# Another order for the half products of an MLP's down projection, with later weight differences and other banks for the last transposes

## The chip, the cores and the metric

The kernel runs on one core of one Trainium2 chip, as one launch. The metric is the device time of a whole execution in microseconds (us), lower is better. All data are float32.

## What is computed

A decoder trunk of two layers on 512 tokens of width 1024. In each layer a normalised input goes through one wide projection and three token mixers (latent attention, RWKV-7, short convolution), whose gated sum goes through an output projection into the residual. Then comes the MLP, which the change touches:

```python
h2 = rms_norm(x, mlp_norm[l])
x = x + jnp.square(jax.nn.relu(h2 @ w_up[l])) @ w_down[l]      # w_up 1024 x 4096, w_down 4096 x 1024
```

## The kernel before

**Exact products from two halves.** TensorE multiplies in a reduced float32 format (fp32r). So every operand is split in a high half, a cast on ACT, and a low half, the rest, a subtraction on DVE. A product of 128 x 128 by 128 x 512 is three matmuls: high by high, high by low, low by high. For weights this happens in split_block (L247 the cast, L248 the low half) and in weights() (L261, L262), for activations in split_into (L339, L340). The halves of weights lie in a ring of four pairs of buffers. Weights come by DMA in blocks of 256 KB, issued on SyncE's queue.

**The MLP in quarters.** Each layer's MLP has four quarters q. A quarter makes 1024 of the 4096 hidden columns: eight up-projection products in the order 0, 4, 1, 5, 2, 6, 3, 7 (UP_ORDER; n_ counts them), each evacuated by two ACT instructions (L1303, L1304). With each of m = 4 to 7 a block j = 0 to 3 of the hidden activations is complete. DVE then forms four half-width sums and differences of it (L1311, L1314, L1312, L1315, in the order in which they stand on DVE), and the results are split.

**Seven half products.** The down projection of a quarter is done in the Strassen-Winograd way: 7 products of quadrants in place of 8. The activations' quadrant operands are A11, S1, S2, S3, S4, A12, A22. The weight quadrants wa, wb, wc, wd hold four blocks each; room gives them the tiles col, kql, ext, z, rstd and mg: wa and wb are col blocks and one kql, wc is three kql and ext, wd is z, z, rstd and mg. These tiles serve the mixers too, under the same names. Three quadrants come by DMA (down_block, L1271). DVE computes wd = wc - wb (L1324) and wb = wb - wa (L1325) once the weights are there. The function less (L1359) makes a further difference of a quadrant while the products run: wc - wb ahead of S2, and the fourth quadrant less wb ahead of A22. The fourth quadrant's own weights are loaded late, into wd, each block after S3's split of that block is done.

Each product is 24 matmuls of 128 x 128 by 128 x 512 (L1344, L1345, L1346) into two PSUM banks, one for each half (t) of 256 tokens: px (pool "g"), pz ("a") or yp ("b"). In program order these are A11 px, S1 pz, S2 px, S3 px, S4 pz, A12 yp, A22 px. What a product leaves in px or pz is added to accumulators ya by add_out: on DVE (L1277), or in an accumulator's first use on ACT (L1279). A product that writes a bank waits until the bank's last result has been added.

**The end of a layer.** In the last quarter the accumulators are finished one by one. finish(b, dh) transposes four 128 x 128 pieces on TensorE into a bank of pool "c" (L1286), DVE adds them to the residual tile am (L1288), and a DMA stores it (L1290) to a spill or the output. In the last quarter A22 runs its two token halves one after the other (by_tokens), with finish(0,0) and finish(1,0) between them.

**What sets the order.** Each engine runs its instructions in the order in which they were put there. A scheduler sets it when the kernel is built, from its own model of times, priorities (tc.high_priority) and the program's order. So an instruction of the MLP can stand among the mixers' work, as the weight differences do: they need only the loaded weights.

Of the kernel before, what the change touches and what calls it, by code (L numbers as in the profile page):

```python
# [22 lines left out]
ALU = mybir.AluOpType  # L23
# [3 lines left out]
P = 128  # L27
# [148 lines left out]
def trunk(tc, w, wkv, wq, xin, pos, pp, sm, rg, out, sizes):  # L176
# [29 lines left out]
    V, A, G = nc.vector, nc.scalar, nc.gpsimd  # L206
# [320 lines left out]
    for l in range(NL):  # L527
# [751 lines left out]
                A.activation(out=ya[b][dh], in_=pd, func=AF.Copy, scale=r_)  # L1279
            seen.add((b, dh))  # L1280

        def finish(b, dh):

            pf = pt("c", (P, 4, P))
            for i in range(4):
                nc.tensor.transpose(pf[:, i], ya[b][dh][:, i * P:(i + 1) * P], ident)  # L1286
            part = xt[:, 4 * dh:4 * dh + 4, b * P:(b + 1) * P]
            V.tensor_tensor(out=part, in0=pf, in1=part, op=ALU.add)  # L1288
            dst = xd if l < NL - 1 else out
            nc.sync.dma_start(out=dst.rearrange("p (k t) -> p k t", t=T)[:, 4 * dh:4 * dh + 4, b * P:(b + 1) * P], in_=part)  # L1290

        for q in range(4):
# [3 lines left out]
            for n_, m in enumerate(UP_ORDER):  # L1296
                pu = pt("c")
                run(gemm_steps(pu, None, h2), h2_steps if (q, n_) == (0, 1) else None)
                if (q, n_) == (0, 2):
                    r2 = const.tile([P, NB], F32, name=f"r2_{l}")  # L1300
                    V.tensor_tensor(out=r2, in0=h2_at[0], in1=h2_at[0], op=ALU.mult)
                rl = tl("inv")
                A.activation(out=rl, in_=pu, func=AF.Relu)  # L1303
                A.activation(out=rl, in_=rl, func=AF.Square)  # L1304
                us[m] = rl
                if m >= 4:
                    j = m - 4
                    ua, ub = us.pop(j), us.pop(m)
                    split_into(act["A11", j], ua[:, H1])
                    s12, s34 = tl("inv"), tl("inv")  # L1310
                    V.tensor_tensor(out=s12[:, H1], in0=ua[:, H2], in1=ub[:, H2], op=ALU.add)  # L1311
                    V.tensor_tensor(out=s12[:, H2], in0=s12[:, H1], in1=ua[:, H1], op=ALU.subtract)  # L1312
                    split_into(act["S1S2", j], s12)
                    V.tensor_tensor(out=s34[:, H1], in0=ua[:, H1], in1=ua[:, H2], op=ALU.subtract)  # L1314
                    V.tensor_tensor(out=s34[:, H2], in0=ub[:, H1], in1=s12[:, H2], op=ALU.subtract)  # L1315
                    split_into(act["S3S4", j], s34)
                    split_into(act["A12A22", j], ub)

                if n_ < 6:
                    for i in (2 * n_, 2 * n_ + 1):  # L1320
                        down_block(i, (wa + wb + wc)[i])
                elif n_ == 6:
                    for j in range(4):
                        V.tensor_tensor(out=wd[j], in0=wc[j], in1=wb[j], op=ALU.subtract)  # L1324
                        V.tensor_tensor(out=wb[j], in0=wb[j], in1=wa[j], op=ALU.subtract)  # L1325
            wpos[0], wpos[1] = first + 32, sum(sizes[:first + 32]) * P
            px, pz = [pt("g") for _ in range(2)], [pt("a") for _ in range(2)]

            def product(a, blocks, acc, start, outs, before=None, after=None, by_tokens=False):

                ws = {}
                for t, j in [(t, j) for t in range(2) for j in range(4)] if by_tokens else \
                        [(t, j) for j in range(4) for t in range(2)]:
                    if j not in ws:
                        if before:
                            before(j)
                        ws[j] = split_block(blocks[j])
                        if after:
                            after(j)
                    hi, lo = ws[j]  # L1340
                    ah, al = act[a, j]
                    c = slice(t * P, (t + 1) * P)

                    mm(acc[t], ah[:, c], hi, start=(start and j == 0), stop=False, skip_group_check=True)  # L1344
                    mm(acc[t], ah[:, c], lo, start=False, stop=False, skip_group_check=True)  # L1345
                    mm(acc[t], al[:, c], hi, start=False, stop=(j == 3), skip_group_check=True)  # L1346
                    if by_tokens and j == 3:
                        for th, dh in outs:
                            add_out(acc[t], 2 * th + t, dh)
                        if t == 0:  # L1350
                            finish(0, 0)
                            finish(1, 0)
                if not by_tokens:
                    for t in range(2):
                        for th, dh in outs:
# [6 lines left out]
            product("A11", wa, px, True, [(0, 0)])  # L1362
            product("S1", wb, pz, True, [(1, 1)])
            product("S2", wb, px, False, [(0, 1)], before=less(wb, wc, wb))
            product("S3", wd, px, False, [(1, 1)], after=lambda j: down_block(12 + j, wd[j]))
            product("S4", wc, pz, False, [(0, 1)])
            if last:
                finish(2, 1)
                finish(3, 1)
            product("A12", wd, yp, q == 0, [(0, 0)] if last else [])  # L1370
            if last:
                finish(0, 1)
                finish(1, 1)
            product("A22", wb, px, False, [(1, 0)], before=less(wb, wd, wb), by_tokens=last)
        finish(2, 0)
        finish(3, 0)
        xsrc = xd
    es.close()

# [18 lines left out]
```

## Time and profile before

| | |
|---|---|
| median of 3 runs | 1577.67 us (1577.0 to 1578.12) |
| profiled execution | 1579.63 us |
| its span, first to last instruction | 1577.6 us |
| TensorE (PE) busy | 1559.8 us, 99% |
| DVE busy | 1179.4 us, 75% |
| ACT busy | 797.2 us, 51% |
| GpSimd (POOL) busy | 182.2 us, 12% |
| granted TensorE clock | 0.999 |
| moved by DMA | 156.27 MB, 99 GB/s on the mean |

How to read it: PE is TensorE's matmuls, PEld its weight loads, SPq SyncE's DMA queue. A timeline's row has the start, the duration, the engine, the line, the operation and its tiles (out<-in), and in brackets how long the engine was idle before it and what released it. The duration of a matmul is longer than the distance of two starts, since matmuls are pipelined and their ends are modelled. A waits' row has the total in us, the count and the longest.

### The profile page before, as it was taken

Reading aid. Unit: us, or ns where it says so; the run is one execution under the profiler, and the core shown is the slowest. Engines: PE = TensorE matmul, PEld = TensorE weight load, DVE = VectorE, ACT = ScalarE, POOL = GpSimd, SP = SyncE. Lnnn points to the kernel's source line nnn. Section 1 sums busy time; section 2 is a strip of 40 time slices with the busy share of each in tenths; the row PEclk is TensorE's granted clock in tenths of the full one; section 3 lists DMA queues with packets and bytes.
Section 4 is the critical chain, followed back from the end, with each engine's and each line's share of the span. In section 5 each row is a group of like instructions: output and inputs, shape, how many; then the busy total and the mean of one; then the engine's idle time right before and its main releaser. Section 6 shows DMA issues by size and latency. Waiting matters only on the chain.

```text
span 1577.6 us, 22682 instructions
## 1 busy us (share of the span) xinstructions
PE 1559.8 (99%) x7910; PEld 1259.6 (80%) x7910; DVE 1179.4 (75%) x2351; ACT 797.2 (51%) x1708; POOL 182.2 (12%) x192
## 2 busy tenths in 40 slices
PE   9999999999999999999999999999999999999998
PEld 7888778877788888878777887788778888788786
DVE  8889677688756767686968996776887576776767
ACT  5433556454446554646434335654544565646462
POOL 1312014101100000000022221151111000000000
PEclk9999999999999999999999999999999999999999
DMA  5323324314332424242233243242143324242412
GB/s 180 98 74 112 113 71 143 89 41 167 101 96 79 127 73 133 81 121 67 69 107 92 81 135 93 65 141 74 54 165 98 97 77 128 73 132 74 127 34 80
DMA packets 90786, 156.27 MB, mean 99 GB/s; under 512 B 10032, under 2 KB 20272, under 8 KB 90160
## 3 DMA queue, kind: packets, MB, share of 16 engines
q1 hardware_dynamic: 90672, 154.83, 32.8%
q8 instruction: 62, 1.02, 0.3%
q14 instruction: 52, 0.43, 0.1%
HBM read 145.87 MB, written 8.91 MB: 98 GB/s over the span
## 4 chain that ended last, share of the span: by engine, by line
PE 91%; DVE 5%; DMA 2%; ACT 1%; issue 0%; SPq 0%; DVEq 0%
PE pg L298 12%; PE pg L300 12%; PE pg L302 12%; PE pc L300 7%; PE pc L298 7%; PE pc L302 7%; PE pg L1344 3%; PE pg L1345 3%; PE pg L1346 3%; PE pa L1171 2%; PE pa L1345 1%; PE pa L1346 1%; PE pa L1344 1%; DVE mg L1277 1%; DVE lo L248 1%; PE pc L1197 1%
## 5 line engine op out<-in xcount | busy, mean ns | idle before, releaser
L261 ACT CAST hi<-raw 128x512 fp32r<-128x512 f32 (+1 forms) x366 | 224.6, 618 | 332.7 <-PE pg L300 150.0
L262 DVE TENSOR_TENSOR lo<-raw,hi 128x512 fp32r<-128x512 f32 (+1 forms) x366 | 264.7, 725 | 123.9 <-ACT hi L261 122.0
L300 PE MATMUL pg<-xg,hi 128*128 128x512 f32 x608 | 246.9, 406 | 0.0
L298 PE MATMUL pg<-xg,hi 128*128 128x512 f32 x608 | 245.4, 404 | 0.7 <-DVE z L611 0.7
L302 PE MATMUL pg<-xg,lo 128*128 128x512 f32 x608 | 241.0, 396 | 0.0
L302 PE MATMUL pc<-xg,lo 128*128 128x512 f32 x512 | 199.4, 389 | 0.0
L300 PE MATMUL pc<-xg,hi 128*128 128x512 f32 x512 | 199.2, 389 | 0.0
L298 PE MATMUL pc<-xg,hi 128*128 128x512 f32 x512 | 199.2, 389 | 0.0
L298 PEld LDWEIGHTS pg<-xg,hi 128*128 128x128 f32 x608 | 114.3, 188 | 28.5 <-issue 3.0
L302 PEld LDWEIGHTS pg<-xg,lo 128*128 128x128 f32 x608 | 114.4, 188 | 26.2 <-issue 3.4
L300 PEld LDWEIGHTS pg<-xg,hi 128*128 128x128 f32 x608 | 114.4, 188 | 25.7 <-issue 3.4
L300 PEld LDWEIGHTS pc<-xg,hi 128*128 128x128 f32 x512 | 96.1, 188 | 20.1
L298 PEld LDWEIGHTS pc<-xg,hi 128*128 128x128 f32 x512 | 96.1, 188 | 20.0
L302 PEld LDWEIGHTS pc<-xg,lo 128*128 128x128 f32 x512 | 96.1, 188 | 19.8
L247 ACT CAST hi<-col 128x512 fp32r<-128x512 f32 x104 | 64.6, 621 | 78.9 <-PE pc L300 30.8
L248 DVE TENSOR_TENSOR lo<-col,hi 128x512 fp32r<-128x512 f32 x104 | 71.4, 688 | 34.2 <-ACT hi L247 33.7
L345 POOL TENSOR_TENSOR t<-t,mhalf 128x4 f32<-128x4 f32 (+1 forms) x26 | 46.3, 1783 | 228.1 <-DVE t L356 201.3
L1175 ACT ACTIVATE inv<-pa,t 128x128 f32<-128x128 f32 (+3 forms) x64 | 33.7, 527 | 47.6 <-DVE t L1173 46.1
L247 ACT CAST hi<-kql 128x512 fp32r<-128x512 f32 x48 | 29.8, 622 | 34.3 <-PE pg L1346 24.9
L665 POOL TENSOR_TENSOR mg<-mg,z 128x512 f32<-128x512 f32 x16 | 22.8, 1426 | 180.8 <-DVE z L618 180.8
L612 ACT ACTIVATE z<-z 128x512 f32<-128x512 f32 x48 | 30.3, 632 | 25.0 <-DVE z L611 16.1
L611 DVE TENSOR_TENSOR z<-pg,rstd 128x512 f32<-128x512 f32 x48 | 33.0, 687 | 13.0 <-PE pg L302 10.0
(468 smaller groups left out, 3452.4 us busy)
## 6 DMA issues: line engine op xcount, KB each, us to landing
raw<-in_w_dram SPq DMA_DIRECT2D x364, 256.0 KB, 2.6
col<-in_w_dram SPq DMA_DIRECT2D x56, 256.0 KB, 2.7
kql<-in_w_dram SPq DMA_DIRECT2D x32, 256.0 KB, 2.7
z_spill<-z SPq DMA_DIRECT2D x16, 256.0 KB, 3.3
inv<-z_spill SPq DMA_DIRECT2D x16, 256.0 KB, 5.7
z<-in_w_dram SPq DMA_DIRECT2D x16, 256.0 KB, 2.7
raw<-in_wq_dram SPq DMA_DIRECT2D x12, 192.0 KB, 2.3
am<-in_x_dram SPq DMA_DIRECT2D x8, 256.0 KB, 5.6
```

What stands on the lines that cost most here:

```text
L247: A.copy(hi, src)
L248: V.tensor_tensor(out=lo, in0=src, in1=hi, op=ALU.subtract)
L261: A.copy(hi[:, c], raw[:, c])
L262: V.tensor_tensor(out=lo[:, c], in0=raw[:, c], in1=hi[:, c], op=ALU.subtract)
L298: mm(dst, hi[:, c0:c0 + P], ah, start=(k == 0), stop=False)
L300: mm(dst, hi[:, c0:c0 + P], al, start=False, stop=False)
L302: mm(dst, lo[:, c0:c0 + P], ah, start=False, stop=(k == n - 1))
L345: G.tensor_tensor(out=y, in0=v, in1=mhalf.to_broadcast([P, n]), op=ALU.pow)
L1175: A.activation(out=pe[:, 0:n], in_=psc[:, 0:n], func=AF.Exp, bias=nm[:, h:h + 1], accum_out=rsum[:, h:h + 1])
L1344: mm(acc[t], ah[:, c], hi, start=(start and j == 0), stop=False, skip_group_check=True)
L1345: mm(acc[t], ah[:, c], lo, start=False, stop=False, skip_group_check=True)
L1346: mm(acc[t], al[:, c], hi, start=False, stop=(j == 3), skip_group_check=True)
```

## The change

Four edits, all in the MLP:

1. The program order of the half products becomes A11, S1, S2, S4, S3, A12, A22, with the same banks. The fourth quadrant's weights are loaded into wc, after S4's splits, and A12 and A22's difference use wc.
2. The eight differences of a quarter (now L1327 and L1328) may be issued only after the first difference of block j = 2 (mark).
3. In the last quarter finish(0,1) and finish(1,1) stand before A12, finish(2,1) and finish(3,1) after it; finish(1,0) moves from the middle of A22 to its end. The last three transposes take banks of pools "a", "c", "a"; finish(0,0) keeps "c".
4. finish's add on DVE (now L1289) has high priority.

The lines behind an edit move: the four differences of a block L1311, L1314, L1312, L1315 are L1312, L1315, L1313, L1316 after, the matmuls L1344 to L1346 are L1347 to L1349, and less's L1359 is L1361.

```diff
-        def finish(b, dh):
+        def finish(b, dh, pst="c"):
-            pf = pt("c", (P, 4, P))
+            pf = pt(pst, (P, 4, P))
...
-            V.tensor_tensor(out=part, in0=pf, in1=part, op=ALU.add)
+            with tc.high_priority():
+                V.tensor_tensor(out=part, in0=pf, in1=part, op=ALU.add)
...
-                    V.tensor_tensor(out=s12[:, H1], in0=ua[:, H2], in1=ub[:, H2], op=ALU.add)
+                    mark = V.tensor_tensor(out=s12[:, H1], in0=ua[:, H2], in1=ub[:, H2], op=ALU.add)
...
                 elif n_ == 6:
-                    for j in range(4):
-                        V.tensor_tensor(out=wd[j], in0=wc[j], in1=wb[j], op=ALU.subtract)
-                        V.tensor_tensor(out=wb[j], in0=wb[j], in1=wa[j], op=ALU.subtract)
+                    with tc.issue_after(mark.ins):
+                        for j in range(4):
+                            V.tensor_tensor(out=wd[j], in0=wc[j], in1=wb[j], op=ALU.subtract)
+                            V.tensor_tensor(out=wb[j], in0=wb[j], in1=wa[j], op=ALU.subtract)
...
                         if t == 0:
                             finish(0, 0)
-                            finish(1, 0)
...
             product("S2", wb, px, False, [(0, 1)], before=less(wb, wc, wb))
-            product("S3", wd, px, False, [(1, 1)], after=lambda j: down_block(12 + j, wd[j]))
-            product("S4", wc, pz, False, [(0, 1)])
+            product("S4", wc, pz, False, [(0, 1)], after=lambda j: down_block(12 + j, wc[j]))
+            product("S3", wd, px, False, [(1, 1)])
+            if last:
+                finish(0, 1)
+                finish(1, 1)
+            product("A12", wc, yp, q == 0, [(0, 0)] if last else [])
             if last:
                 finish(2, 1)
                 finish(3, 1)
-            product("A12", wd, yp, q == 0, [(0, 0)] if last else [])
-            if last:
-                finish(0, 1)
-                finish(1, 1)
-            product("A22", wb, px, False, [(1, 0)], before=less(wb, wd, wb), by_tokens=last)
-        finish(2, 0)
-        finish(3, 0)
+            product("A22", wb, px, False, [(1, 0)], before=less(wb, wc, wb), by_tokens=last)
+        finish(1, 0, "a")
+        finish(2, 0, "c")
+        finish(3, 0, "a")
```

**DVE in the third block.** The rows are from the second quarter of layer 0, where block j = 2 is formed (inv_6000 and inv_6001 are its sums and differences, mix, prep, ar hold the halves of the activations, col_4987 on are blocks of wa). Before:

```order
L1311 TENSOR_TENSOR inv_6000<-inv_5953,inv_5995 128x256
L1314 TENSOR_TENSOR inv_6001<-inv_5953 128x256
L1312 TENSOR_TENSOR inv_6000<-inv_6000,inv_5953 128x256
L340 TENSOR_TENSOR ar_4974<-inv_5995,ar_4973 128x512
L1315 TENSOR_TENSOR inv_6001<-inv_5995,inv_6000 128x256
L248 TENSOR_TENSOR lo_6121<-col_4987,hi_6120 128x512
L340 TENSOR_TENSOR prep_4971<-inv_6000,prep_4970 128x512
L340 TENSOR_TENSOR ar_4973<-inv_6001,prep_4972 128x512
L248 TENSOR_TENSOR lo_6131<-col_4988,hi_6130 128x512
L340 TENSOR_TENSOR ar_4974<-inv_6051,ar_4974 128x256
```

and after:

```order
L1327 TENSOR_TENSOR z_4999<-kql_4995,col_4991 128x512
L1327 TENSOR_TENSOR z_5000<-kql_4996,col_4992 128x512
L1327 TENSOR_TENSOR rstd_5001<-kql_4997,col_4993 128x512
L1327 TENSOR_TENSOR mg_5002<-ext_4998,kql_4994 128x512
L1313 TENSOR_TENSOR inv_6000<-inv_6000,inv_5953 128x256
L340 TENSOR_TENSOR ar_4974<-inv_5995,ar_4973 128x512
L248 TENSOR_TENSOR lo_6121<-col_4987,hi_6120 128x512
L1328 TENSOR_TENSOR col_4991<-col_4991,col_4987 128x512
L1328 TENSOR_TENSOR col_4992<-col_4992,col_4988 128x512
L1328 TENSOR_TENSOR col_4993<-col_4993,col_4989 128x512
L1328 TENSOR_TENSOR kql_4994<-kql_4994,col_4990 128x512
L1316 TENSOR_TENSOR inv_6001<-inv_5995,inv_6000 128x256
```

The eight weight differences stand in two groups of four behind the block's first two differences (L1312, L1315) and between its last two (L1313, L1316); these first two stand just ahead of the rows.

**DVE where S4 and S3 are prepared.** In the same quarter, from the add_out of S2's first bank on (pg_6116 and pg_6117 are px, pa_6118 and pa_6119 are pz; z_4999 to mg_5002 are wd, kql_4995 to ext_4998 are wc, col_4991 to kql_4994 are wb). Before:

```order
L1277 SCALAR_TENSOR_TENSOR mg_4980<-pg_6116,r_0_5149,mg_4980 128x512
L248 TENSOR_TENSOR lo_6273<-rstd_5001,hi_6272 128x512
L1277 SCALAR_TENSOR_TENSOR mg_4982<-pg_6117,r_0_5149,mg_4982 128x512
L1359 TENSOR_TENSOR col_4991<-z_4999,col_4991 128x512
L248 TENSOR_TENSOR lo_6284<-mg_5002,hi_6283 128x512
L1359 TENSOR_TENSOR col_4992<-z_5000,col_4992 128x512
L1359 TENSOR_TENSOR col_4993<-rstd_5001,col_4993 128x512
L248 TENSOR_TENSOR lo_6297<-kql_4995,hi_6296 128x512
L248 TENSOR_TENSOR lo_6307<-kql_4996,hi_6306 128x512
L1359 TENSOR_TENSOR kql_4994<-mg_5002,kql_4994 128x512
L1277 SCALAR_TENSOR_TENSOR mg_4984<-pg_6116,r_0_5149,mg_4984 128x512
L248 TENSOR_TENSOR lo_6317<-kql_4997,hi_6316 128x512
```

and after:

```order
L1277 SCALAR_TENSOR_TENSOR mg_4980<-pg_6116,r_0_5149,mg_4980 128x512
L248 TENSOR_TENSOR lo_6273<-kql_4997,hi_6272 128x512
L1277 SCALAR_TENSOR_TENSOR mg_4982<-pg_6117,r_0_5149,mg_4982 128x512
L1361 TENSOR_TENSOR col_4991<-kql_4995,col_4991 128x512
L248 TENSOR_TENSOR lo_6284<-ext_4998,hi_6283 128x512
L1361 TENSOR_TENSOR col_4992<-kql_4996,col_4992 128x512
L248 TENSOR_TENSOR lo_6297<-z_4999,hi_6296 128x512
L1361 TENSOR_TENSOR col_4993<-kql_4997,col_4993 128x512
L248 TENSOR_TENSOR lo_6307<-z_5000,hi_6306 128x512
L1361 TENSOR_TENSOR kql_4994<-ext_4998,kql_4994 128x512
L1277 SCALAR_TENSOR_TENSOR mg_4980<-pa_6118,r_0_5149,mg_4980 128x512
L248 TENSOR_TENSOR lo_6317<-rstd_5001,hi_6316 128x512
```

The add_outs of S2 keep their place. S4's low halves stand where S3's were and S3's where S4's were, and the differences for A22 (L1361) now stand between S3's low halves.

**DVE at the layer change.** From add_out of (2,0) on (mg_4983; mg_4985 is (3,0)); xg, inv and raw belong to the next layer's start. Before:

```order
L1277 SCALAR_TENSOR_TENSOR mg_4983<-pg_7524,r_0_5149,mg_4983 128x512
L1288 TENSOR_TENSOR am_4586<-pc_7849,am_4586 128x4x128
L326 SCALAR_TENSOR_TENSOR xg_7891<-am_4586,pp_82,xg_7890 128x512
L1288 TENSOR_TENSOR am_4586<-pc_7856,am_4586 128x4x128
L384 TENSOR_TENSOR inv_7927<-inv_7923,inv_7925 128x512
L326 SCALAR_TENSOR_TENSOR xg_7895<-am_4586,pp_82,xg_7894 128x512
L262 TENSOR_TENSOR lo_7959<-raw_7957,hi_7958 128x512
L384 TENSOR_TENSOR inv_7931<-inv_7927,inv_7929 128x512
L1277 SCALAR_TENSOR_TENSOR mg_4985<-pg_7525,r_0_5149,mg_4985 128x512
```

and after:

```order
L1277 SCALAR_TENSOR_TENSOR mg_4983<-pg_7524,r_0_5149,mg_4983 128x512
L1289 TENSOR_TENSOR am_4586<-pc_7849,am_4586 128x4x128
L326 SCALAR_TENSOR_TENSOR xg_7891<-am_4586,pp_82,xg_7890 128x512
L384 TENSOR_TENSOR inv_7927<-inv_7923,inv_7925 128x512
L326 SCALAR_TENSOR_TENSOR xg_7895<-am_4586,pp_82,xg_7894 128x512
L262 TENSOR_TENSOR lo_7959<-raw_7957,hi_7958 128x512
L1277 SCALAR_TENSOR_TENSOR mg_4985<-pg_7525,r_0_5149,mg_4985 128x512
L384 TENSOR_TENSOR inv_7931<-inv_7927,inv_7929 128x512
L1289 TENSOR_TENSOR am_4586<-pa_7869,am_4586 128x4x128
```

The add_out of (3,0) stands two rows further forward: one final add and one L384 that stood ahead of it now follow it.

**DVE at the end of layer 1's attention.** L618 and L340 belong to the mixers' sum, raw and lo to its weights; z, rstd, col and kql in the rows L1324 and L1325 are the first quarter's weights. Before:

```order
L1202 TENSOR_TENSOR prep_11119<-pc_12026,prep_11118 128x128
L1324 TENSOR_TENSOR z_12677<-kql_12673,col_12669 128x512
L618 SCALAR_TENSOR_TENSOR inv_12057<-inv_12057,pg_12059 128x512
L1325 TENSOR_TENSOR col_12669<-col_12669,col_12665 128x512
L262 TENSOR_TENSOR lo_12157<-raw_12155,hi_12156 128x512
L1324 TENSOR_TENSOR rstd_12678<-kql_12674,col_12670 128x512
L618 SCALAR_TENSOR_TENSOR inv_12083<-inv_12083,pg_12085 128x512
L340 TENSOR_TENSOR ar_12073<-mg_9780,ar_12073 128x512
L1325 TENSOR_TENSOR col_12670<-col_12670,col_12666 128x512
L262 TENSOR_TENSOR lo_12184<-raw_12182,hi_12183 128x512
L618 SCALAR_TENSOR_TENSOR inv_12109<-inv_12109,pg_12111 128x512
```

and after:

```order
L1202 TENSOR_TENSOR prep_11119<-pc_12026,prep_11118 128x128
L618 SCALAR_TENSOR_TENSOR inv_12057<-inv_12057,pg_12059 128x512
L262 TENSOR_TENSOR lo_12157<-raw_12155,hi_12156 128x512
L618 SCALAR_TENSOR_TENSOR inv_12083<-inv_12083,pg_12085 128x512
L340 TENSOR_TENSOR ar_12073<-mg_9780,ar_12073 128x512
L262 TENSOR_TENSOR lo_12184<-raw_12182,hi_12183 128x512
L618 SCALAR_TENSOR_TENSOR inv_12109<-inv_12109,pg_12111 128x512
```

The rows L1324 and L1325 are gone from between the mixers' rows; the same rows are gone from layer 0's attention.

## The prediction

> **What bounds the kernel now.** I read the page first: the busy shares and the engines of the chain that ended last.
>
> ```profile
> PE 1559.8 (99%) x7910; PEld 1259.6 (80%) x7910; DVE 1179.4 (75%) x2351; ACT 797.2 (51%) x1708; POOL 182.2 (12%) x192
> PE 91%; DVE 5%; DMA 2%; ACT 1%; issue 0%; SPq 0%; DVEq 0%
> ```
>
> TensorE sets the time, and the change leaves its matmuls in number and size as they are. So only TensorE's standstills can go, and they are short. Next I read PE's own waits (columns: us in total, times, longest):
>
> ```profile
> PE pg L1344 <- DVE mg L1277: 2.9, 12, 0.3
> PE pc L1286 <- DVE mg L1277: 2.2, 2, 1.8
> ```
>
> Twelve waits of the products' first matmuls (L1344) for add_out (L1277) are two in each of six quarters: the first quarter of a layer has no L1277 yet. The timeline shows what such a wait costs in full. Here is PE in the second quarter of layer 0, at the end of S1 (bank pa), in S2 (pg), and where S3 (pg again) begins:
>
> ```profile
> 586.53 0.39 PE L1344 MATMUL pa<-hi,ar 128*128 128x512 f32 x1
> 587.02 0.50 PE L1345 MATMUL pa<-lo,ar 128*128 128x512 f32 x1
> ...
> 588.31 0.39 PE L1344 MATMUL pg<-hi,mix 128*128 128x512 f32 x1
> ...
> 591.05 0.39 PE L1344 MATMUL pg<-hi,prep 128*128 128x512 f32 x1
> 591.35 0.50 PE L1345 MATMUL pg<-lo,prep 128*128 128x512 f32 x1
> ...
> 593.79 0.40 PE L1346 MATMUL pg<-hi,ar 128*128 128x512 f32 x1
> 594.42 0.47 PE L1344 MATMUL pg<-hi,mix 128*128 128x512 f32 x1 [0.24 <-DVE mg L1277]
> 594.73 0.39 PE L1345 MATMUL pg<-lo,mix 128*128 128x512 f32 x1
> 594.95 0.40 PE L1346 MATMUL pg<-hi,mix 128*128 128x512 f32 x1
> 595.59 0.50 PE L1344 MATMUL pg<-hi,mix 128*128 128x512 f32 x1 [0.24 <-DVE mg L1277]
> 595.93 0.39 PE L1345 MATMUL pg<-lo,mix 128*128 128x512 f32 x1
> ```
>
> Durations overlap, so I count start to start. S2's 23 steps from 588.31 to 593.79 take 5.48 us, stall included, so an undisturbed step is about 0.23. Of the stalls, (a) is 587.02 - 586.53 - 0.23 = 0.26, where PE wants the low half (L248) of S1's fourth weight block; (b) is 0.30 - 0.23 = 0.07, for the low half of S2's third block; (c) is the S2-to-S3 change: 0.63, 0.31, 0.64 and 0.34 less 0.23 each, 0.40 + 0.08 + 0.41 + 0.11 = 1.00 us. A matmul after a stall also comes about 0.1 late, so (a) and (b) count 0.11 more each, 0.55 together. In the first quarter of a layer add_out runs on ACT (L1279), and (c) is smaller:
>
> ```profile
> 511.06 0.39 PE L1346 MATMUL pg<-hi,ar 128*128 128x512 f32 x1
> 511.55 0.50 PE L1344 MATMUL pg<-hi,mix 128*128 128x512 f32 x1
> ```
>
> 0.49 - 0.23 = 0.26, and 0.11 behind it: 0.37.
>
> **The change part by part. The order S1, S2, S4, S3.** S4 writes the pair pz, whose last owner S1 was evacuated long before, as DVE's rows of that quarter show (the x2 row holds both):
>
> ```profile
> 586.29 0.68 DVE L248 TENSOR_TENSOR lo<-kql,hi 128x512 fp32r<-128x512 f32 x1
> ...
> 589.29 1.40 DVE L1277 SCALAR_TENSOR_TENSOR mg<-pa,r,mg 128x512 f32<-128x512 f32 x2
> 590.62 0.68 DVE L248 TENSOR_TENSOR lo<-col,hi 128x512 fp32r<-128x512 f32 x1
> ...
> 593.53 0.75 DVE L1277 SCALAR_TENSOR_TENSOR mg<-pg,r,mg 128x512 f32<-128x512 f32 x1 [0.42 <-PE pg L1346]
> ```
>
> Start to start, an add_out takes 0.66 (two of them fill 589.29 to 590.62) and a full-width row of 0.68 takes 0.60. S1's banks are free at 590.69, and S4 now wants them at 593.79 + 0.23 = 594.02. S3 wants S2's banks 24 steps later, at 599.5, and their add_outs start at 593.53 and, one low half later, 594.79, so 3 us are to spare. (c) goes: 6 x 1.00 + 2 x 0.37 = 6.74 us. I assume that the four quarters whose rows I do not quote are alike, as the count of 12 and the total of 2.9 (0.24 each) say.
>
> On what weights load during a stall, the row at 595.93 shows 0.11 lost behind the wait. The Trainium skill, "TensorE: Matmul & The Clock Gate", "Step-by-step: what each phase is for", says that the queue pulls weight loads ahead of matmuls in flight, so the wait alone should cost; by that rule (c) would be 0.81 a quarter and the term 6 x 0.81 + 2 x 0.26 = 5.4. The row decides for 6.74.
>
> (a) and (b) bring nothing. From the fourth block's first difference to the low half at 590.62, DVE's rows hold the same 21 instructions before and after, only permuted; that low half ends when it did. The order frees the low half behind (a) by one L340 (0.60), so (a) goes and (b) grows by as much: 0 (bounds 0 and 8 x 0.55 = 4.4, if the queue were to start earlier, for which I see no reason).
>
> **The eight differences held back.** They now stand on DVE in the third block (j=2), all behind the up-projection's last low half. From that block's first L1311 to the next one's, DVE has this room:
>
> ```profile
> 651.23 0.42 DVE L1311 TENSOR_TENSOR inv<-inv,inv 128x256 f32<-128x256 f32 x1 [0.47 <-ACT inv L1304]
> ...
> 662.11 0.43 DVE L1311 TENSOR_TENSOR inv<-inv,inv 128x256 f32<-128x256 f32 x1 [0.47 <-ACT inv L1304]
> ```
>
> 10.88 us. In it stand after the change 4 x 0.34 (L1312 to L1316, 0.42 less the same 0.08) + 8 x 0.60 (the differences) + 7 x 0.60 (four low halves, three L340) + 0.43 (a half-width L340) = 10.79. It fits with 0.09 to spare: cost 0, and any us beyond costs one, in each of eight quarters, since (b) has no slack.
>
> What they leave behind matters too: in layer 1's attention they stand in front of work that PE waits for.
>
> ```profile
> 1175.98 0.69 DVE L1324 TENSOR_TENSOR rstd<-kql,col 128x512 f32<-128x512 f32 x1 [1.50 <-DMA col<-in_w_dram]
> 1176.59 0.68 DVE L618 SCALAR_TENSOR_TENSOR inv<-inv,pg 128x512 f32<-128x512 f32 x1
> ...
> 1177.33 0.50 PE L298 MATMUL pg<-prep,hi 128*128 128x512 f32 x1 [0.76 <-DVE inv L618]
> ...
> 1180.92 0.47 PE L298 MATMUL pg<-prep,hi 128*128 128x512 f32 x1 [0.57 <-ACT hi L261]
> ```
>
> An idle figure in brackets counts from the modelled end, 0.39 - 0.23 = 0.16 behind the step, so the two stalls are 0.92 and 0.73, with about 0.1 behind each: 1.85. Six differences (3.6 us) and the wait of 1.50 leave the queue there. I take 1.6, since the low halves and L618 stay and can each leave a piece (bounds 0 and 1.85).
>
> **The reload into the other tiles.** S4's four reloads (L1271) now follow S4's low halves, on the DVE rows where S3's stood. The differences that wait for them now stand ahead of S3's low halves, and S3's are needed by PE. The transfer, and how DVE met the fourth block's reload before (the wait's row is for all eight quarters, the two starts are those of the second and third quarter):
>
> ```profile
> ext<-in_w_dram SPq DMA_DIRECT2D x8, 256.0 KB, 2.8
> ...
> DVE kql L1359 <- DMA mg<-in_w_dram: 3.4, 3, 1.8
> ...
> 600.20 0.68 DVE L1359 TENSOR_TENSOR kql<-mg,kql 128x512 f32<-128x512 f32 x1
> ...
> 684.63 0.69 DVE L1359 TENSOR_TENSOR kql<-mg,kql 128x512 f32<-128x512 f32 x1 [1.83 <-DMA mg<-in_w_dram]
> ```
>
> The fourth block's low half stands four rows behind the add_out at 593.53, so 0.66 + 0.60 + 0.66 + 0.60 later, at 596.05, and ends at 596.73. Its reload lands 2.8 later, 599.5; the difference takes 0.60, add_out 0.66, S3's third low half 0.68: 601.5. PE wants that one 13 steps into S3, at 599.5 + 13 x 0.23 = 602.5. So 1.0 us is to spare, and at the median nothing is lost. PE stands once the difference starts behind 599.5 + 1.0 = 600.5. Before, its turn came at 600.20, and in three of the eight quarters it waited beyond that, 3.4 in all. If the same lateness came again, 3.4 - 3 x 0.3 = 2.5 would be lost; I take half of it, 1.2, since which reloads are late is nothing that the trace ties to a place (bounds 0 and 2.5; more is a rival).
>
> **The layer change.** PE's finish(3,0) waits 1.77 (the larger part of the 2.2 above) for an add_out late in DVE's queue:
>
> ```profile
> 784.72 0.68 DVE L1288 TENSOR_TENSOR am<-pc,am 128x512 f32<-128x512 f32 x1
> 785.32 0.68 DVE L384 TENSOR_TENSOR inv<-inv,inv 128x512 f32<-128x512 f32 x1
> ...
> 787.19 0.68 DVE L384 TENSOR_TENSOR inv<-inv,inv 128x512 f32<-128x512 f32 x1
> 787.79 0.74 DVE L1277 SCALAR_TENSOR_TENSOR mg<-pg,r,mg 128x512 f32<-128x512 f32 x1
> ...
> 788.59 0.66 PE L1286 MATMUL pc<-ident,mg 128*128 128x128 f32 x4 [1.77 <-DVE mg L1277]
> ```
>
> The order puts this add_out ahead of one final add (0.60, as from 784.72 to 785.32) and one L384 (0.60, from 787.19 to 787.79): 1.20 earlier (bounds 0.6 and 1.9, the whole stall).
>
> **The end.** PE is done about 0.4 earlier, since one group of four transposes fewer stands in A22. But behind the last add_out stand three final adds, where two stood of which one came before it:
>
> ```profile
> 1572.00 0.75 DVE L1277 SCALAR_TENSOR_TENSOR mg<-pg,r,mg 128x512 f32<-128x512 f32 x1 [1.68 <-PE pg L1346]
> ...
> 1573.50 0.69 DVE L1288 TENSOR_TENSOR am<-pc,am 128x512 f32<-128x512 f32 x1 [0.15 <-PE pc L1286]
> ...
> DMA to landing us min/median/max: 2.3/2.3/3.2
> ```
>
> 1572.00 - 0.4 + 0.66 + 2 x 0.60 = 1573.5 for the last add's start, as before. Three output transfers are then under way where two were: -0.1 (bounds 0 and -0.9, the slowest landing against the median).
>
> Sum: 6.74 + 1.6 + 1.2 - 0.1 - 1.2 = 8.24 us. The profiled execution took 1579.63 (span 1577.6 and 2.0 around it); it becomes 1571.4. The median of the runs, 1577.67, lies 1.96 under the profiled one, so I forecast 1569.4, 0.52% faster.
>
> **The rivals.** One: the chain on DVE slips (slower). Its place is the third block: the second difference L1313 now stands behind four of the held ones, so ACT's cast of it (L339) starts 2.4 us later, and DVE's own L340 waits for ACT behind it. With 0.09 us of room, each us of that wait is a us of PE in eight quarters; it decides from 8.24 / 8 = 1.0 us on. At 1.5 the time is 1569.4 + 8 x 1.5 = 1581.4. For it speaks that the room is so small; against it that ACT is 51% busy and that rows of other work stand between the difference and its L340. Chance 0.05.
>
> Two: the bank wait turns into a reload wait. If in six of the eight quarters the fourth block's reload is as late as at 684.63 (1.83 - 0.3 = 1.5 of PE each), 9.0 is lost in place of 1.2: 1569.4 - 1.2 + 9.0 = 1577.2, no change. For it speak the three waits; against it that five quarters had none, and that the two others shared 1.6. The Trainium skill, "DMA: Bandwidth & Descriptors", "Latency and other measured facts", gives 0.2 us for a memory access on average and 2 at high load; by that a reload under load would be 1.8 late (an estimate from that page), which the row at 684.63 shows once and the medians do not. Chance 0.07.
>
> Three: DVE is the bound of the products, and (c) comes back as late low halves.
>
> ```profile
> 577.00:615.60 38.60, 38.02 (x164) 30.24 (x163) 33.68 (x56) 19.28 (x32) 0.00 (x0) 1.00 0.32 95
> ```
>
> DVE (the third figure) is busy 33.68 of a quarter's 38.60 us of products, and without the stalls 33.68 of 37.0: 91%. Against it: after 590.62 DVE idles 0.42 at 593.53 and has its low halves ahead of PE. With all of the six quarters' (c) back, 1569.4 + 6.0 = 1575.4. Chance 0.08.
>
> That the change does not do what it says is ruled out by the order of the rows. My forecast keeps 0.80.
>
> **How the numbers follow.** The low end takes every gain at its bound but (a) and (b), and no late reload: 6.74 + 1.85 + 1.9 = 10.5, 1567.2; and 2 us more for a part of (a) and (b): 1565.2. The high end gives back the larger loss of reloads (1.3), all of the attention's gain (1.6), half of the layer change's (0.6) and a quarter of (c) (1.6): 1569.4 + 5.1 = 1574.5. It reaches part of the third rival; the first, the second and the rest are 0.17. About 0.2% (3.2 us) is what a measurement of this kernel can tell from no change, so faster means under 1574.5: my forecast's 0.80 and a third of the third rival, 0.83; same is the second rival and most of the rest, 0.13; slower 0.04.
>
> **What would show it.** In the profile of the changed kernel PE's waits should list no L1347 for L1277 in quarters two to four; S1's last low half should no longer stall PE, and S2's third should by about 0.45; DVE's next block should start within 0.1 us of ACT's L1304; finish(3,0) should wait about 0.6 rather than 1.77; no stall of 0.9 should stand at L298 after 1170. It is wrong if PE's steps in S3 or S4 show new gaps for L248, or if L1361 waits over 1 us for reloads in most quarters.

## The result, and the profile after

The changed kernel takes 1568.38 us (median of 4 runs, 1567.12 to 1569.6) where the kernel before takes 1577.55 (4 runs, 1577.0 to 1578.12). The ratio is 0.9938, with a 95% interval of 0.9926 to 0.9949: 9.2 us, 0.58% faster. The profiled execution took 1569.6 us with a span of 1567.9. The forecast was 1569.4. The changed kernel was measured once more beside the experiments: 10.6 us faster, a ratio of 0.9931 (0.9917 to 0.9945), and the two intervals overlap.

PE's own waits in the profile after, as in the prediction (us in total, times, longest):

```profile
PE pg L1348 <- DVE lo L248: 3.3, 8, 1.0
...
PE pa L1286 <- DVE mg L1277: 0.6, 1, 0.6
```

The twelve waits for L1277 at a product's start are gone, and of the 2.2 us at the transposes 0.6 are left. In their place stand eight waits for a low half. Here is PE in the second quarter of layer 0: S1's last block (pa), S2's third block (pg), and the start of S4 (pa).

```profile
585.22 0.39 PE L1347 MATMUL pa<-hi,ar 128*128 128x512 f32 x1
585.44 0.39 PE L1348 MATMUL pa<-lo,ar 128*128 128x512 f32 x1
...
589.30 0.39 PE L1347 MATMUL pg<-hi,prep 128*128 128x512 f32 x1
590.03 0.50 PE L1348 MATMUL pg<-lo,prep 128*128 128x512 f32 x1 [0.35 <-DVE lo L248]
590.37 0.40 PE L1349 MATMUL pg<-hi,prep 128*128 128x512 f32 x1
...
592.43 0.39 PE L1349 MATMUL pg<-hi,ar 128*128 128x512 f32 x1
592.66 0.39 PE L1347 MATMUL pa<-hi,mix 128*128 128x512 f32 x1
592.88 0.39 PE L1348 MATMUL pa<-lo,mix 128*128 128x512 f32 x1
```

From S2 to S4 (592.43 to 592.66) there is a plain step of 0.23: (c) is gone. So is (a), from 585.22 to 585.44. The place of (b) has grown: 590.03 - 589.30 - 0.23 = 0.50, and 0.11 behind it, 0.61 in all where (a) and (b) together were 0.55. From A11's first matmul to S2's 17th, the same instructions of PE in both profiles, each of the six quarters takes as long as before to 0.02 us.

Two of the eight waits stand elsewhere, in S3's third block. The worst is in the third quarter of layer 0. First DVE, then PE at the same place:

```profile
679.35 0.68 DVE L248 TENSOR_TENSOR lo<-z,hi 128x512 fp32r<-128x512 f32 x1
682.41 0.69 DVE L1361 TENSOR_TENSOR kql<-ext,kql 128x512 f32<-128x512 f32 x1 [2.37 <-DMA ext<-in_w_dram]
683.02 0.74 DVE L1277 SCALAR_TENSOR_TENSOR mg<-pa,r,mg 128x512 f32<-128x512 f32 x1
683.68 0.68 DVE L248 TENSOR_TENSOR lo<-rstd,hi 128x512 fp32r<-128x512 f32 x1
...
684.41 0.50 PE L1348 MATMUL pg<-lo,prep 128*128 128x512 f32 x1 [0.97 <-DVE lo L248]
```

A difference for A22 waits 2.37 us for its reload, and the low half of rstd, which PE needs, stands two rows behind it. In the last quarter of layer 1 it is the third block's reload, 1.76 us late, and PE stands 0.7 in S3. That is the second rival's mechanism, in two quarters instead of six.

The held differences fit the third block as the row of before said. DVE, second quarter of layer 0, from the block's first difference to the next block's:

```profile
566.61 0.43 DVE L1312 TENSOR_TENSOR inv<-inv,inv 128x256 f32<-128x256 f32 x1 [0.47 <-ACT inv L1305]
...
576.72 0.68 DVE L248 TENSOR_TENSOR lo<-col,hi 128x512 fp32r<-128x512 f32 x1
577.49 0.43 DVE L1312 TENSOR_TENSOR inv<-inv,inv 128x256 f32<-128x256 f32 x1
```

577.49 - 566.61 = 10.88 as before. The last row could be followed 0.60 behind its start, at 577.32, so 0.17 us are to spare.

The layer change, at finish(3,0), where 1.77 stood:

```profile
784.08 0.66 PE L1286 MATMUL pa<-ident,mg 128*128 128x128 f32 x4 [0.56 <-DVE mg L1277]
```

The end, the last output transfers alone (L1290 before, L1291 after; issues from the first to the last, then how long behind its issue a transfer landed):

```profile
L1290 SPq DMA_DIRECT2D out_dram<-am x2: 372/372/372, 1573.4 to 1574.2; - x2
DMA to landing us min/median/max: 2.3/2.4/2.4
...
L1291 SPq DMA_DIRECT2D out_dram<-am x3: 372/372/373, 1562.7 to 1563.9; - x3
DMA to landing us min/median/max: 2.3/2.6/2.9
```

The prediction took 3.2 us for the slowest landing at the end. That figure counts all sixteen transfers of finish, and the slow ones are spills at the layer change, in the kernel before and in every other. At the end the last of two transfers landed in 2.4, the last of three in 2.9.

### The profile page after: what moved, and what is told of

The parts are those of the page before. It is cut to its first block, busy times and chain, and to the rows that moved or that the text cites. A ratio compares the mean times of both kernels' runs of the same rounds, so it can differ in the third digit from the quotient of the medians.

```text
span 1567.9 us, 22646 instructions
## 1 busy us (share of the span) xinstructions
PE 1552.2 (99%) x7910; PEld 1261.9 (80%) x7910; DVE 1173.8 (75%) x2351; ACT 796.5 (51%) x1708; POOL 184.7 (12%) x192
## 4 chain that ended last, share of the span: by engine, by line
PE 90%; DVE 7%; DMA 1%; ACT 1%; issue 0%; SPq 0%; DVEq 0%
PE pg L298 13%; PE pg L300 13%; PE pg L302 12%; PE pc L300 7%; PE pc L298 7%; PE pc L302 7%; PE pg L1348 3%; PE pg L1349 2%; PE pa L1171 2%; PE pg L1347 2%; DVE lo L248 2%; DVE mg L1277 1%; PE pc L1197 1%; PE pb L1185 1%; PE pb L1349 1%; PE pb L1348 1%
## 5 line engine op out<-in xcount | busy, mean ns | idle before, releaser
L261 ACT CAST hi<-raw 128x512 fp32r<-128x512 f32 (+1 forms) x366 | 224.6, 618 | 333.2 <-PE pg L300 145.4
L262 DVE TENSOR_TENSOR lo<-raw,hi 128x512 fp32r<-128x512 f32 (+1 forms) x366 | 269.3, 736 | 147.7 <-ACT hi L261 142.5
L248 DVE TENSOR_TENSOR lo<-col,hi 128x512 fp32r<-128x512 f32 x104 | 70.9, 683 | 9.3 <-ACT hi L247 8.8
L247 ACT CAST hi<-kql 128x512 fp32r<-128x512 f32 x72 | 44.1, 621 | 46.1 <-PE pg L1349 35.8
L248 DVE TENSOR_TENSOR lo<-kql,hi 128x512 fp32r<-128x512 f32 x72 | 47.7, 684 | 8.2 <-ACT hi L247 8.0
L1277 DVE SCALAR_TENSOR_TENSOR mg<-pg,r,mg 128x512 f32<-128x512 f32 x52 | 38.8, 745 | 10.7 <-PE pg L1349 10.5
```

Of the source, the lines that this page charges most:

```text
L247: A.copy(hi, src)
L248: V.tensor_tensor(out=lo, in0=src, in1=hi, op=ALU.subtract)
L261: A.copy(hi[:, c], raw[:, c])
L262: V.tensor_tensor(out=lo[:, c], in0=raw[:, c], in1=hi[:, c], op=ALU.subtract)
L1277: V.scalar_tensor_tensor(out=ya[b][dh], in0=pd, scalar=r_, in1=ya[b][dh], op0=ALU.mult, op1=ALU.add)
```

## The experiments

Every run was timed in five rounds beside the kernel before on the same chip, which there had medians of 1578.8 to 1579.1 us, so the ratios, and differences within one chip, carry the verdicts. Ahead of the first column of layer 0's attention output, where no edit reaches, PE of these profiles is up to 0.7 us before or behind PE of the kernel before; the figures of a stage below are taken between two instructions of PE behind that. A column is one 128 x 512 piece of the attention's output stage.

**The order alone.** Of the change only the order of the products, the reload into wc and the finishes that follow the order:

```diff
-            product("S3", wd, px, False, [(1, 1)], after=lambda j: down_block(12 + j, wd[j]))
-            product("S4", wc, pz, False, [(0, 1)])
+            product("S4", wc, pz, False, [(0, 1)], after=lambda j: down_block(12 + j, wc[j]))
+            product("S3", wd, px, False, [(1, 1)])
...
```

> The kernel before with the new order of the half products and the reload into wc alone: no held differences, transposes and final adds as before. My theory: the bank wait between products goes (7.1 us in the eight quarters), late reloads give about 1.7 back: 1572.2 us, and PE has no wait for L1277 at a product's start in quarters two to four. The attention stages keep their stalls. Rival, that DVE bounds the products and the gain came from the held differences: 1576 to 1578, with new waits for low halves (L248) in S4 or S3 of most quarters.

Measured: 1572.19 us, 0.9958 (0.9946 to 0.9971) of the kernel before on that chip (1579.09), 6.6 to 6.9 us. PE's waits list no L1277 at a product's start; at the same instructions of PE the product stages are 0.41 ahead in each layer's first quarter and 0.99 to 1.07 in the six others, 7.0 in all. The attention stages keep their stalls: at 1176.72 PE still waits 0.57 for L261. That the time lies on the expected 1572.2 is luck: that figure stood for a gain of 5.4 (7.1 less 1.7), the kernel before took about 1.5 more on this chip than in the first measurement, and late reloads cost 0.3 in place of 1.7. The weights that the attention's differences wait for also came at other times: layer 1's wait was 0.67 in place of 1.50 and its attention 0.8 shorter, layer 0's 0.3 longer, with no edit there. The order alone is two thirds of the change, and the rival that DVE bounds the products falls for this load.

**The hold alone.** Of the change only the mark and the issue_after:

```diff
+                    with tc.issue_after(mark.ins):
...
```

> The kernel before with the eight differences held behind the mark alone. My theory after the result: both attention stages gain, 1.1 us in layer 0 and 2.6 in layer 1, and the products lose nothing: 1573.9 us, bank waits as before (12, 2.9 us). Rival 1, the term of my prediction (only layer 1, 1.6): 1576.0. Rival 2, the held differences make DVE late in the third block: S2's stall for L248 grows in eight quarters, 1578 or more.

Measured: 1575.09, 0.9976 (0.9967 to 0.9985), 4.0 us. Between the same instructions of PE, layer 0's attention is 1.10 shorter and layer 1's 2.67; the products keep their twelve bank waits (2.9 us), and (a) moves to (b) without a gain or a loss. My term of 1.6 for layer 1 alone was too small. DVE at the first three columns of layer 0's attention that have an add on GpSimd beside them:

```profile
387.65 0.69 DVE L618 SCALAR_TENSOR_TENSOR inv<-inv,pg 128x512 f32<-128x512 f32 x1 [1.26 <-PE pg L302]
...
390.38 0.69 DVE L618 SCALAR_TENSOR_TENSOR inv<-inv,pg 128x512 f32<-128x512 f32 x1 [1.43 <-PE pg L302]
...
393.29 0.68 DVE L618 SCALAR_TENSOR_TENSOR inv<-inv,pg 128x512 f32<-128x512 f32 x1
```

DVE is early and waits for PE here. From then on it takes 2.9 a column (393.29 - 390.38 = 2.91), and no step of PE in the columns of either layer is more than 0.03 us longer than a plain one.

**No GpSimd beside DVE.** The kernel before, with the mixers' last adds on DVE for all columns:

```diff
-                (V if m > 5 else G).tensor_tensor(out=mg[m], in0=mg[m], in1=z, op=ALU.add)
+                V.tensor_tensor(out=mg[m], in0=mg[m], in1=z, op=ALU.add)
```

> The kernel before with the mixers' last adds (L1228) of all eight columns on DVE, where six of them ran on GpSimd. Theory: the small stalls of 0.18 us a column in the attention's output stage come from DVE rows that take 1.78 us in place of 0.68 when GpSimd runs beside them; DVE then needs 2.9 us a column where PE needs 2.72. Without GpSimd DVE needs 4 x 0.60 = 2.4, the rows of 1.78 are gone, and layer 0 gains 1.1, layer 1 0.5 to 1.0 (the wait for a DMA stays): about 1575.7 us. Rival: the long rows have another cause and an add of 0.6 more on DVE makes a column 3.5: 10 us slower.

Measured: 1576.98, 0.9986 (0.9977 to 0.9995), 2.1 us. The reason is in the rows of two columns. The kernel before, DVE in layer 0's attention, then GpSimd (POOL) at the same time:

```profile
394.38 0.68 DVE L618 SCALAR_TENSOR_TENSOR inv<-inv,pg 128x512 f32<-128x512 f32 x1
394.97 0.68 DVE L262 TENSOR_TENSOR lo<-raw,hi 128x512 fp32r<-128x512 f32 x1
395.57 1.79 DVE L340 TENSOR_TENSOR ar<-mg,ar 128x512 fp32r<-128x512 f32 x1
397.28 0.68 DVE L618 SCALAR_TENSOR_TENSOR inv<-inv,pg 128x512 f32<-128x512 f32 x1
...
395.19 1.61 POOL L1228 TENSOR_TENSOR mg<-mg,inv 128x512 f32<-128x512 f32 x1 [1.90 <-DVE inv L618]
398.10 1.60 POOL L1228 TENSOR_TENSOR mg<-mg,inv 128x512 f32<-128x512 f32 x1 [1.29 <-DVE inv L618]
```

And this run's DVE:

```profile
397.60 0.68 DVE L618 SCALAR_TENSOR_TENSOR inv<-inv,pg 128x512 f32<-128x512 f32 x1
398.20 0.68 DVE L262 TENSOR_TENSOR lo<-raw,hi 128x512 fp32r<-128x512 f32 x1
398.80 0.69 DVE L340 TENSOR_TENSOR ar<-mg,ar 128x512 fp32r<-128x512 f32 x1
399.40 0.68 DVE L1228 TENSOR_TENSOR mg<-mg,inv 128x512 f32<-128x512 f32 x1
400.00 0.68 DVE L618 SCALAR_TENSOR_TENSOR inv<-inv,pg 128x512 f32<-128x512 f32 x1
```

A DVE row that runs while L1228 runs on GpSimd takes 1.79 in place of 0.68. A column then costs DVE 397.28 - 394.38 = 2.90; without GpSimd it costs 400.00 - 397.60 = 2.40, with one instruction more. PE needs 12 steps, 2.72. So before, DVE loses 0.18 a column, and once it is late PE stands 0.15 at each column. In this run these stalls are gone but for 0.3 in one column of each layer; the sum of 2.1 holds 2.2 gained in layer 1, and in layer 0 0.8 gained and 1.1 lost, the loss at a difference that still waits for its weights:

```profile
391.58 0.69 DVE L1324 TENSOR_TENSOR rstd<-kql,col 128x512 f32<-128x512 f32 x1 [2.02 <-DMA col<-in_w_dram]
```

The rival (10 us slower) falls. That the two layers came out other than expected (1.1, 0.5 to 1.0) is this wait: which layer it hits differs. Of layer 1's 2.2, 1.0 stands where PE waits behind that difference (its wait was 1.01 here, 1.50 before), and the order alone gained 0.8 there with the adds on GpSimd. So by the profile the adds account for 0.8 in layer 0 and about 1.2 in layer 1.

**S1's adds later.** The changed kernel, with the two add_outs of S1 behind S2's last low half. In the profile of after, S2's third low half has these adds in front of it, and nobody waits for them:

```diff
-            product("S1", wb, pz, True, [(1, 1)])
+            s1_adds = product("S1", wb, pz, True, [(1, 1)], late=True)
             product("S2", wb, px, False, [(0, 1)], before=less(wb, wc, wb))
+            with tc.issue_after(newest[0].ins):
+                s1_adds()
...
```

(newest is the last low half of split_block; with late, product returns its adds instead of making them.)

> The changed kernel with the two add_outs of S1 (L1277) put behind S2's last low half, where two of S2's low halves were behind them. Theory: the one stall left in quarters two to four, 0.62 us at S2's third low half, is only this order on DVE, 1.33 us of adds that nobody waits for; it goes in six quarters, 3.7 us: 1564.7 us. Rival, DVE's throughput bounds the products: the stall comes back at S4's or S3's low halves, 1568 us.

Measured: 1567.06, 0.9925 (0.9912 to 0.9937). No stall is left at S2 in six quarters, 0.64 each. But in the first quarter of a layer the adds run on ACT, and there S4 waits for them. PE, layer 0:

```profile
509.63 0.39 PE L1351 MATMUL pg<-hi,ar 128*128 128x512 f32 x1
511.38 0.50 PE L1349 MATMUL pa<-hi,mix 128*128 128x512 f32 x1 [1.36 <-ACT mg L1281]
```

1.63 us twice, so 3.3 of the 3.8 were lost again. Neither theory had this. The mended edit keeps the first quarter (late=q > 0). It ran beside the changed kernel unaltered:

> The changed kernel unaltered, on the same chip as the next three, as their base. 0.9938 of the kernel before, within the interval of the first measurement; late reloads in one to three quarters.

> The run with S1's adds behind S2's last low half gained 0.64 us in each of six quarters but lost 1.63 in the first quarter of each layer, where add_out runs on ACT. Here the first quarters keep the order of the changed kernel. Theory: the gain of 6 x 0.64 = 3.8 us stays and the loss of 3.3 goes: 3.8 us under the changed kernel on this chip. Rival, DVE's throughput: under 2 us.

Measured: the changed kernel 1568.19, 0.9931 (0.9917 to 0.9945); with the adds late 1563.78, 0.9902 (0.9887 to 0.9918), 4.4 us less. PE's waits for L248:

```profile
PE pg L1350 <- DVE lo L248: 0.2, 1, 0.2
```

One is left of eight. By the profile the six quarters are 3.8 shorter up to S2's third block. The rest of the 4.4 goes with the reloads: PE's 1.1 in S3 of layer 0's third quarter is gone as well, whether by this edit isn't shown, and the last quarter of layer 1 keeps 0.6. So (b), in which (a) had gone under, is no limit of DVE's throughput; it is 1.33 us of adds in the wrong place.

**A22's differences later.** The changed kernel, with the differences that wait for the reload held behind S3's last low half (s3_lo):

```diff
+            def less_late(j):
+                with tc.issue_after(s3_lo.ins):
+                    V.tensor_tensor(out=wb[j], in0=wc[j], in1=wb[j], op=ALU.subtract)
...
-            product("A22", wb, px, False, [(1, 0)], before=less(wb, wc, wb), by_tokens=last)
+            product("A22", wb, px, False, [(1, 0)], before=less_late, by_tokens=last)
```

> The changed kernel with A22's four differences of a quarter, which wait for the reload, held behind S3's last low half. Theory: PE's waits in S3's third block come only from a late reload ahead of S3's low half; they go (1.64 us in the changed kernel's profile, 0.3 in that of the order alone, so 0 to 1.7 by the lateness of the run): 0.5 to 1.6 us under the changed kernel, and no gap at S3's third low half in any quarter. Rival: the differences then come late themselves or make A12's low halves late: no gain, new gaps at A12 or A22.

Measured: 1567.38, 0.9927 (0.9914 to 0.994), 0.8 less than the changed kernel on that chip, which is within the intervals; the profile decides:

```profile
PE pg L1350 <- DVE lo L248: 2.1, 6, 0.4
```

Six waits, all (b); the two in S3 are gone (1.13 in the third quarter of layer 0 and 0.50 in the last of layer 1, between the same instructions of PE). The changed kernel had them in the same two places in both its profiles. So they were reloads. Their places recur, but not their sizes: on DVE the one in layer 0's third quarter was 2.37 and 2.21 in the changed kernel's two profiles and 0.66 in that of the run with finish(1,0) in the middle, where PE loses nothing there though no edit touches these products. With this edit none is left in three profiles, but one profile doesn't price it.

**One more difference.** The changed kernel, with the first held difference made twice:

```diff
+                        V.tensor_tensor(out=wd[0], in0=wc[0], in1=wb[0], op=ALU.subtract)
```

> The changed kernel with one of the held differences made twice (the first, written to the same tile), 0.60 us more on DVE in the third block of each quarter. By the prediction's row the block has 0.09 us of room, so the next block starts 0.51 late, and S2's third low half with it: 6 x 0.51 = 3.1 us slower than the changed kernel in the six quarters that have that stall, less or nothing in the two that have none (the prediction said eight: 4.1). Rival, DVE has more room than the rows say: no change.

Measured: 1571.67, 0.9954 (0.9941 to 0.9967), 3.5 us more than the changed kernel. DVE and PE in the second quarter of layer 0:

```profile
566.79 0.43 DVE L1312 TENSOR_TENSOR inv<-inv,inv 128x256 f32<-128x256 f32 x1 [0.47 <-ACT inv L1305]
...
578.11 0.41 DVE L1312 TENSOR_TENSOR inv<-inv,inv 128x256 f32<-128x256 f32 x1
...
590.65 0.50 PE L1349 MATMUL pg<-lo,prep 128*128 128x512 f32 x1 [0.56 <-DVE lo L248]
```

The next block starts 11.32 behind, 0.44 more than 10.88, so 0.60 of work met a room of 0.16, and PE is 0.43 to 0.49 behind in each of six quarters, 2.6 by the profile; the other 0.9 of the times is inside the intervals. The two first quarters lose nothing.

**finish(1,0) in the middle again**, in the changed kernel:

```diff
                         if t == 0:
                             finish(0, 0)
+                            finish(1, 0)
...
-        finish(1, 0, "a")
```

> The changed kernel with finish(1,0) back between the token halves of A22, in both layers; the final adds keep their high priority, the banks of the last two transposes stay c and a. Theory: the layer change's gain and the end's loss both come from this one step. DVE then has a final add and an L384 ahead of add_out(3,0) again, so PE's stall at finish(3,0) is 1.9 again where the changed kernel has 0.7 (1.2 us slower); and at the end two output transfers are under way in place of three, which land in 3.2 after the issue in place of 3.6 (0.4 faster). Net 0.5 to 0.9 slower than the changed kernel. Rival: the layer change's gain comes from the high priority or the banks: no stall of 1.9.

Measured: 1568.89, 0.9938 (0.9924 to 0.9951): 0.7 over the changed kernel's 1568.19 (the kernels before took 1578.83 and 1578.8 beside them), inside the intervals. In the profile the layer change is 1.21 longer, at the wait that the change had shortened:

```profile
783.81 0.66 PE L1286 MATMUL pa<-ident,mg 128*128 128x128 f32 x4 [1.77 <-DVE mg L1277]
```

So that gain is the place of finish(1,0), neither the priority nor the banks. The half on the end came out too: the last of two output transfers landed in 2.4, and from A12's last matmul to the end of the span this kernel takes as long as the kernel before, 0.5 less than the changed one. The 3.2 and 3.6 of the expectation are the slowest spills of the layer change.

**Both moves, and the last finish.** S1's adds late in quarters two to four and A22's differences late; then also finish(1,0) in the middle in the last layer alone:

```diff
+                            if l == NL - 1:
+                                finish(1, 0)
...
-        finish(1, 0, "a")
+        if l < NL - 1:
+            finish(1, 0, "a")
```

> The changed kernel with both moves: S1's adds behind S2's last low half in quarters two to four, and A22's differences behind S3's last low half. Theory: the two stalls are independent, 4.0 + 0.8 to 1.6: 0.9870 to 0.9885 of the kernel before, 0.003 under the changed kernel's ratio at least, and PE has no wait for a low half (L248) in any product. Rival: the DVE rows that are moved back collide in S4 and S3: no better than S1's adds alone (0.9902).

> The run before, and finish(1,0) in the middle of A22 in the last layer alone, where no next layer waits for it. Theory: 0.4 us less at the end by two output transfers in place of three, which the times hardly tell and the last landing does (3.2 us in place of 3.6 to 3.7); the layer change stays at 0.7. Rival: the landing depends on something else: 3.6 again.

Measured: 1563.11, 0.9901 (0.9888 to 0.9915), and 1562.91, 0.9900 (0.9886 to 0.9913). The us of the first expectation fit (5.1 under the changed kernel's 1568.19, where 4.8 to 5.6 were written); the ratio written beside them was a slip, since 4.8 of 1578.8 from 0.9931 is 0.9901. Against S1's adds alone the second move is worth 0.7, not told from none by the intervals; in the profile no product has a wait for L248 left. The last finish gave 0.2 by the times, not told from none. In the profile the stretch from A12's last matmul to the end of the span is 0.5 shorter than in the run before, and the last output landed in 2.4 in place of 2.9. The fastest of all kernels is this one, 15.9 us under the kernel before on that chip.

## Why the prediction was right, step by step

The sizes are from the profiles before and after, between the same instructions of PE.

| step | predicted | measured | run that shows it |
|---|---|---|---|
| (c), six quarters and two | 6.74 | 7.1 | the order alone: 7.0 |
| (a) moves into (b) | 0 | 0.0 | the hold alone: 0; S1's adds late: 3.8 by moving the adds |
| held differences, products | 0 | 0 | the hold alone: 0; one more: 2.6 lost |
| held differences, attention | 1.6 | 3.8 (1.1 and 2.7) | the hold alone: 1.10 and 2.67 |
| late reloads | -1.2 | -1.9 (-1.6 in the repeat) | A22's differences late: both gone |
| layer change | 1.2 | 1.2 | finish(1,0) in the middle: -1.21 |
| the end | -0.1 | -0.5 | finish(1,0) in the middle: gone |

The sum is 9.7 where 8.24 was forecast. The spans of the two profiles differ by 9.7, the medians by 9.2. The time came out 1.0 us under the forecast because the attention's term was too small by 2.2, and its size lies outside its own bound of 1.85. (c) brought 0.4 more, and late reloads and the end took 0.7 and 0.4 back. That the total is so near is in part luck.

**The attention.** I counted the two large waits (0.92 and 0.73) and left pieces for L618 and the low halves. The step that was missing is the reserve of a slow queue: DVE needs 2.90 a column and PE 2.72, so DVE falls behind by 0.18 in each column with an add on GpSimd, and a late start shows in every column that follows. The differences used up the reserve; without them DVE waits for PE at the first two such columns (1.26 and 1.43 in the hold alone), and all pass before that is gone. The two large waits brought 1.8 of the 3.8, near the forecast; the columns brought 1.1 in layer 0, where no wait was long enough to be listed, and 0.9 in layer 1. DVE's wait for weights in layer 1 (1.50 in the kernel before, 0.67 and 1.01 in two other runs that have it) differs by run, so layer 1's share does too.

**The second stall.** That (a) only moves into (b) held in each run that holds the differences back and leaves S1's adds in place, but for the one with one more difference. The bound of 4.4 that I gave "if the queue were to start earlier" and saw no reason for has one: not an earlier start, but two adds fewer in front, worth 3.8 in the six quarters that have the stall. I had taken the queue's contents as given.

**Eight quarters or six.** The price of a late third block was put at one us for one us in eight quarters; it is about that in six (0.44 late, 0.43 to 0.49 lost). The room itself was written as 0.09, because one half-width L340 stood in the sum at 0.43 where the other half-width rows stood at 0.34; counted alike it is 0.18, and the runs show 0.16 to 0.17. The first quarter of a layer has no adds on DVE and so no stall there.

**The rivals.** The first (a late chain) did not occur, since DVE kept its room; the run with one more difference shows that its price for a quarter was right. The second occurred in two quarters. The third falls: with S1's adds and A22's differences late the low halves come in time everywhere, at the same work on DVE.

**The page's rule on weight loads.** The Trainium skill, "TensorE: Matmul & The Clock Gate", "Step-by-step: what each phase is for", says that weight loads are pulled ahead of matmuls in flight; by that a stall should cost only its wait, and the prediction had 5.4 for (c) by it. The measured 7.0 to 7.1 sides with the rows, which show 0.08 to 0.11 more behind every stall, here and in each experiment. In the kernel before, the weight load of the matmul that waits at 511.55 starts with it, where the load of the matmul at 510.84 had started 0.22 ahead.

**The end.** The step was right, three output transfers under way in place of two, and its size was not. The three are issued 0.6 us apart and land 0.9 apart (1562.7 + 2.3, 1563.9 + 2.9), so the last one lands 0.5 later behind its issue than the last of two. In the seven profiles with three the last landed in 2.9, in the six with two in 2.4.

**What stays open.** Why the reload is late in just two of eight quarters, the fourth block's in one and the third block's in the other, and why its lateness differs from run to run, wasn't tried. It cost PE 1.9 and 1.6 us in the changed kernel's two profiles. Why three transfers land 0.9 apart wasn't tried either.

## What to carry to other kernels

When a wait goes, look at what stands in front of the next late instruction in its engine's queue, and ask of each row who waits for it: here two adds that nobody needed yet cost 3.8 us, more than half of what the change brought by its new order. Work moved out of another stage's queue gives back more than the waits in the list where that queue is slower per step than its consumer, so compare the two periods. And a move that is free on one engine has its price on the other: the same adds, late on ACT, cost 1.63 us each time.

## What the runs showed of the hardware

- The first 128 x 512 DVE operation that started while the GpSimd add of that size (L1228) ran took 1.77 to 1.79 us in place of 0.68. L340, L262 and L1325 did so, whichever stood there, twelve times in the two attention stages of the kernel before, and none with the adds on DVE. The operation that DVE had begun before the add kept its 0.68.
- Behind each stall of TensorE in the products and the columns the next step was 0.08 to 0.11 us longer than 0.23.
- Three output transfers of 256 KB that were issued 0.6 us apart landed 0.9 apart, the last 2.9 behind its issue; two that were issued 0.8 apart landed in 2.3 and 2.4.
